# A two-block network on one core: split buffers, later transposes and a mirrored half inverse transform in the context branch

## The chip, the cores and the metric

One core of a Trainium2 chip runs the whole program. The time is device microseconds of one execution, all loads from HBM included. Lower is better.

## The reference

The network has two blocks, each of 256 positions by 1024 features, and a context of the same size beside each.

The first block has two layers. A layer is a token mixer (an mLSTM with four heads in two directions, a depthwise convolution of width 31 and a 2-D Fourier mix, each on a part of the projected features, then an output projection) and an expert layer, in which each of 16 experts takes its 32 best tokens:

```
xs = xn[idx]                                  # 32 tokens of each expert
hid = silu(xs @ w_gate[e]) * (xs @ w_up[e])
y[idx] += gate * (hid @ w_down[e])
```

In layer 0 the context stream goes through both parts as well; in layer 1 it only gives the mLSTM its start states.

The second block first runs a Hyena mixer, on the latents and, separately, on a second context `ctx_2`; then an attention over both. The Hyena mixer of one sequence h of length 256 is:

```
x0, x1, v, z = split(h @ w_in)   # the first three through a convolution of width 3
u = x1 * v
y = irfft(rfft(u, 512) * rfft(k, 512))[:256] + u * d_skip
out = (y * x0 * silu(z)) @ w_out
```

A gate, a shift and a scale for each part come from small vectors times the modulation matrices (`w_ada`, `ada_w_2`). Everything is in 32-bit floats.

## The kernel before

The class `K` writes out the program. `build` asks for a schedule by a simulated timeline (L1589): what the functions write is a program order with dependencies, and the order of the instructions on each engine, fixed when the program is built, may differ from it. Each engine then works its own list. DMA issues are in these lists as well: most on SyncE's queue (SP), those of the context branch on GpSimd's (POOL).

`run` (L1332) goes through these stages: the mixer of layer 0, its routing and experts (with the Hyena filters' spectra `Kd` made beside them), the mixer of layer 1, its routing (`route_tokens`, L701) and experts (`experts`, L825), the context branch of Hyena (`hyena` called with G = 1, `three` False), the latents' Hyena (G = 2, `three` True), attention. Layer 1's experts and the context branch don't depend on each other, so their instructions are interleaved.

An expert of layer 1 is 12 loads of 1 MB (`ew`, L884): four of `w_e_gate`, four of `w_e_up`, four of `w_e_down`. The first six loads go into buffers `W2`, the rest into the five buffers `W` that all stages share. Each load is used by 16 TensorE instructions (`expert_k`, L819) for M = 32 tokens. After gate and up, the hidden row `h` gets its silu on ScalarE and its product on VectorE, is transposed, and goes into the down projection of the same expert.

The context branch works through 16 tiles of 128 channels. For each tile it loads two blocks `Wb` of 1 MB, and makes four projections (`projT`, L266) in the order x1, v, x0, z. A projection splits the weight in two halves, and each half into `hi` (ScalarE cast) and `lo` (VectorE subtraction), with `sbufs` = 2 buffers each; three matmuls per row block (L109 to L111) multiply the pieces with the split input `hyx`, which is X2, the normalized and transposed `ctx_2`. After v, GpSimd forms the even and the odd half `uf` of u (L1058), TensorE transposes them (L1059), ScalarE copies them into `u`; a forward transform with `fe` (four 128-column products), products with the spectrum `Kt` on VectorE (`Yf`, `ht1`), and an inverse transform with `fi`: four products of 256 columns, summed in PSUM. Then `x0s` is multiplied by it and split into `hm`, and after each block of four tiles `out_proj` (L1098) multiplies by `hy_w_out`. The last block, tile 15, is held back until the 15th expert's silu (`late[14]`).

X2 is made inside the context branch (`modulated`, L1092), after the experts in program order. Its pools lie on the right side of the on-chip memory, where the pool of `W2` lay before them.

Modulation parts are named by place (`PLACES`, L28). "a1 b0 b1" are 16 loads of 1 MB of `ada_w_2`, written at `R1`, inside the routing of layer 1. Each load is used by eight TensorE instructions (L191).

Of the kernel before, what the change touches and what calls it, by code (L numbers as in the profile page):

```python
# [27 lines left out]
PLACES = dict(P0="", M0="01 02 10", L0="", R0="a0", W1="", P1="11", M1="12", L1="", R1="a1 b0 b1")  # L28
# [3 lines left out]
class K:  # L32
    def __init__(self, ctx, tc, A, out):
# [15 lines left out]
        self.wgate, self.late = [], {}  # L49

# [275 lines left out]
    def mixer(self, l, x, hc, cols, R, ada):  # L326
# [8 lines left out]
        with self.pool("nrm", tags=("xh", "xtmp")):  # L335
            for s, src in ((0, hc), (1, x)):
                xh = self.normed(src, "og" if s else "xh", 1)
                self.toT(xh, a1, cols[:, 0], s, xhi[:, :, s * 256:s * 256 + 256], xlo[:, :, s * 256:s * 256 + 256],
                         banks=("tp", "sm", "sm", "mm") if s else ("mm", "mm", "mm", "tp"))
# [5 lines left out]
        ott = [0, 1, 2, 3] if full else [2, 3]  # L345
        cum = []
# [78 lines left out]
        flo = T([128, 2, 2, 128], "flo")  # L425
        for s in streams:
# [14 lines left out]
            if s in om:  # L441
                Q[s] = self.parts([128, 1, 256], "Q", 2, True)
# [5 lines left out]
            if s in om:  # L448
# [3 lines left out]
                nc.scalar.activation(flo[:, s], pm, AF.Exp, scale=-1.0)  # L452
# [19 lines left out]
        sgc = T([128, 2, 512], "t4k", 2)  # L472
        ypad = T([128, 2, 2, 286], "ypad")
        nc.vector.memset(ypad[:, :, :, 0:15], 0.0)
        nc.vector.memset(ypad[:, :, :, 271:286], 0.0)
        for h in range(2):
            ps = self.P([128, 512])
            self.projT(ps[:, oc0:], chunk(1 + h), X, oc0, on)
            nc.scalar.activation(sgc[:, h, oc0:], ps[:, oc0:], AF.Sigmoid)
        for h in range(2):  # L480
            ps = self.P([128, 512])
            self.projT(ps[:, oc0:], chunk(3 + h), X, oc0, on)
            for s in om:
                nc.vector.tensor_tensor(ypad[:, h, s, 15:271], ps[:, s * 256:s * 256 + 256],
                                        sgc[:, h, s * 256:s * 256 + 256], op=OP.mult)

        cw, cbias = self.colv["cw", l], self.colv["cb", l]
        acc = T([128, 2, 2, 256], "t4k", 2)
        yo = slice(0, 2) if full else slice(1, 2)

        def terms():
            for j in range(31):
                for h in range(2):
                    av, yv = acc[:, h, yo], ypad[:, h, yo, j:j + 256]
# [10 lines left out]
        qT = T([128, 4, 512], "qT")  # L505
# [4 lines left out]
        for h in range(4):  # L510
            ps = self.P([128, 512])
            self.projT(ps[:, oc0:], chunk(9 + h), X, oc0, on)
            self.copy(qT[:, h, oc0:], ps[:, oc0:])
# [9 lines left out]
        fz = T([128, 4, 256], "t4k", 2)  # L523
# [3 lines left out]
        for q, t in enumerate(ott):  # L527
            self.copy(fz[:, t], pss[q])


        og = T([128, 4, 512], "og")
# [3 lines left out]
        for q, t in enumerate(ott):  # L535
            nc.scalar.activation(og[:, t], pss[q], AF.Sigmoid)
            nc.vector.tensor_tensor(og[:, t], og[:, t], ghn, op=OP.mult)
# [32 lines left out]
        mhi = T([128, 8, 512], "mhi", 1, F32R)  # L570
        mlo = T([128, 8, 512], "mlo", 1, F32R)
# [4 lines left out]
        for s in om:  # L576
            hh[s] = T([128, 4, 2, 128], "hh", 2)
            for h in range(4):
                pS = self.P([128, 2, 256])
                c0 = s * 256  # L580
                for t in range(2):
                    nc.tensor.matmul(pS[:, t], lhsT=kT[:, h, c0 + t * 128:c0 + (t + 1) * 128], rhs=qT[:, h, c0:c0 + 256],
                                     start=True, stop=True)
                for d in range(2):
# [13 lines left out]
                    if s == 1:  # L598
# [5 lines left out]
                        nc.vector.tensor_tensor(qs, qs, qT[:, h, 256:512], op=OP.mult)  # L604
# [12 lines left out]
                    nc.vector.tensor_tensor(rd, rd, flo[:, s, :, r], op=OP.max)  # L617
# [10 lines left out]
            for h in range(4):  # L628
                pt = self.PT([128, 256])
                for t in range(2):  # L630
                    nc.vector.scalar_tensor_tensor(hh[s][:, h, t], hh[s][:, h, t], rsh[:, s, h, t:t + 1],
                                                   og[:, 2 * s + t, h * 128:(h + 1) * 128], op0=OP.mult, op1=OP.mult)
                    nc.tensor.transpose(pt[:, t * 128:(t + 1) * 128], hh[s][:, h, t], self.ident)
                c0 = s * 256
# [4 lines left out]
        for h in range(2):  # L639
            po = self.PT([128, 512])  # L640
            for s in om:
                ps = self.PS([128, 512])
                for t in range(2):
                    nc.tensor.matmul(ps, lhsT=fz[:, 2 * s + t, h * 128:(h + 1) * 128], rhs=fw[:, t], start=(t == 0), stop=(t == 1))
# [5 lines left out]
            nc.scalar.copy(mhi[:, 6 + h, oc0:], po[:, oc0:])  # L650
            nc.vector.tensor_tensor(mlo[:, 6 + h, oc0:], po[:, oc0:], mhi[:, 6 + h, oc0:].bitcast(F32), op=OP.subtract)


        av = acc.rearrange("p h s t -> p h (s t)")[:, :, oc0:]
# [22 lines left out]
        for h in range(2):  # L677
            nc.scalar.activation(av[:, h], av[:, h], AF.Silu, bias=lb[:, h:h + 1], scale=lg[:, h:h + 1])
            nc.scalar.copy(mhi[:, 4 + h, oc0:], av[:, h])
            nc.vector.tensor_tensor(mlo[:, 4 + h, oc0:], av[:, h], mhi[:, 4 + h, oc0:].bitcast(F32), op=OP.subtract)  # L680
# [3 lines left out]
        for n in range(2):  # L684
# [3 lines left out]
            self.projN(wt, (mhi, mlo), ott, 512, pss)  # L688
# [913 lines left out]
```

## Time and profile before

| | |
|---|---|
| median of 3 runs | 2364.46 us (2359.9 to 2367.83) |
| profiled execution, its own time | 2366.99 us |
| its span, first to last instruction | 2365.2 us |
| mean granted clock of TensorE | 0.955 |
| bytes moved | 664.09 MB, 281 GB/s over the span |

The profile is of one execution. Times in a trace are microseconds from the start of its span. A row of the windows gives the busy time of each engine in a stretch, with the number of instructions, then the granted clock (1.00 is 2.4 GHz, 0.50 is 1.2 GHz), the mean busy share of the 16 DMA engines and the rate that they moved. Matmuls are pipelined, so the durations of neighbours overlap.

### The profile page before, as it was taken

The numbers are of one execution on the slowest core, as the hardware profiler recorded it, in microseconds if no ns is written. First come the engines' busy times: TensorE is split into PE (matmuls) and PEld (weight loads), VectorE is DVE, ScalarE is ACT, GpSimd is POOL, SyncE is SP. The second block draws the span as 40 slices with busy tenths as digits, with TensorE's granted clock in tenths as the row PEclk, the third lists the DMA queues.
The fourth block names the chain that finished last, engine by engine and source line by source line (L and its number), as shares of the span: only waits on it lengthen the run. The fifth ranks groups of instructions, "written<-read, shape, count | busy, mean of one in ns | idle before, by whom it ended". The sixth has DMA issues, their size and how long they took to land.

```text
span 2365.2 us, 35049 instructions
## 1 busy us (share of the span) xinstructions
PE 2135.7 (90%) x13966; PEld 1436.1 (61%) x13966; DVE 1250.4 (53%) x2533; ACT 737.5 (31%) x1414; POOL 187.7 (8%) x315
## 2 busy tenths in 40 slices
PE   5999988999999989998799998898777999999998
PEld 3776664343343436864376766665234999979786
DVE  3954444333433337654355555544125878875776
ACT  3323331000000014343233222222013555555665
POOL 1000000011010100000011011100001110100100
PEclk8999999999999999999899999998777999999999
DMA  8247545999999996459799999988996545435320
GB/s 342 99 157 312 204 184 193 413 415 415 414 413 415 414 405 251 137 194 370 295 351 365 372 374 370 351 336 327 421 421 262 185 144 188 168 132 189 126 81 26
DMA packets 129588, 664.09 MB, mean 281 GB/s; under 512 B 12666, under 2 KB 23429, under 8 KB 62352
## 3 DMA queue, kind: packets, MB, share of 16 engines
q1 hardware_dynamic: 115616, 602.89, 66.0%
q0 software_dynamic: 13808, 58.96, 6.6%
q8 instruction: 110, 1.80, 0.3%
q14 instruction: 54, 0.44, 0.1%
HBM read 656.56 MB, written 5.24 MB: 280 GB/s over the span
## 4 chain that ended last, share of the span: by engine, by line
PE 72%; DVE 9%; issue 8%; DMA 7%; ACT 3%; POOL 1%; SPq 0%; DVEq 0%; POOLq 0%; ACTq 0%
PE pmm L823 16%; PE pmm L109 12%; PE pmm L111 11%; PE pmm L110 11%; PE pad L191 3%; PE psm L875 2%; DMA W<-in_w_e_gate 1%; DVE lo L105 1%; DMA W<-in_w_e_up 1%; PE ptp L1017 1%; DMA W<-in_w_ada 1%; PE pmm L798 1%; PE pad L978 1%; DMA W<-in_ada_w 1%; PE ppo L1247 1%
## 5 line engine op out<-in xcount | busy, mean ns | idle before, releaser
L823 PE MATMUL pmm<-W,XS 128*32 128x256 f32 (+1 forms) x3040 | 378.8, 478 | 39.7 <-DMA W<-in_w_e_gate 20.3
L105 DVE TENSOR_TENSOR lo<-W,hi 128x512 fp32r<-128x512 f32 (+1 forms) x420 | 283.7, 680 | 187.1 <-ACT hi L104 184.2
L104 ACT CAST hi<-W 128x512 fp32r<-128x512 f32 (+1 forms) x420 | 255.5, 612 | 352.0 <-PE pmm L110 162.9
L823 PEld LDWEIGHTS pmm<-W,XS 128*32 128x32 f32 (+1 forms) x3040 | 127.0, 123 | 241.3 <-issue 151.1
L823 PE MATMUL pmm<-W,hT 128*32 128x256 f32 (+1 forms) x1536 | 190.1, 483 | 20.2 <-DVE hT L101 8.3
L111 PE MATMUL pmm<-hyx,lo 128*128 128x256 f32 x640 | 191.6, 299 | 10.6 <-DVE lo L105 10.6
L109 PE MATMUL pmm<-hyx,hi 128*128 128x256 f32 x640 | 193.4, 302 | 4.8 <-ACT hi L104 4.8
L110 PE MATMUL pmm<-hyx,hi 128*128 128x256 f32 x640 | 185.8, 290 | 0.0
L105 DVE TENSOR_TENSOR lo<-Wb,hi 128x512 fp32r<-128x512 f32 x160 | 109.4, 692 | 117.3 <-ACT hi L104 116.3
L104 ACT CAST hi<-Wb 128x512 fp32r<-128x512 f32 x160 | 96.8, 619 | 209.4 <-PE pmm L110 138.3
L869 DVE TENSOR_TENSOR Y<-pmm,gt 32x512 f32<-32x512 f32 (+1 forms) x128 | 70.9, 554 | 143.5 <-PE pmm L823 141.8
L109 PE MATMUL pmm<-hyl,hi 128*128 128x256 f32 x512 | 144.5, 283 | 1.7 <-DVE rtmp L697 1.7
L110 PE MATMUL pmm<-hyl,hi 128*128 128x256 f32 x512 | 144.1, 282 | 0.0
L111 PE MATMUL pmm<-hyl,lo 128*128 128x256 f32 x512 | 143.1, 283 | 0.0
L109 PEld LDWEIGHTS pmm<-hyx,hi 128*128 128x128 f32 x640 | 126.6, 198 | 23.7 <-ACT hi L104 16.6
L111 PEld LDWEIGHTS pmm<-hyx,lo 128*128 128x128 f32 x640 | 126.3, 197 | 22.3 <-DVE lo L105 14.1
L823 PEld LDWEIGHTS pmm<-W,hT 128*32 128x32 f32 (+1 forms) x1536 | 65.6, 125 | 117.6 <-issue 68.6
L110 PEld LDWEIGHTS pmm<-hyx,hi 128*128 128x128 f32 x640 | 126.6, 198 | 2.4 <-issue 2.2
L851 ACT ACTIVATE h<-pmm 128x256 f32<-128x256 f32 (+1 forms) x31 | 15.1, 488 | 362.1 <-PE pmm L823 361.9
L191 PE MATMUL pad<-W,cpad 128*32 128x512 f32 x576 | 91.0, 643 | 21.6 <-DMA W<-in_w_ada 16.7
L854 DVE TENSOR_TENSOR h<-h,pmm 128x512 f32<-128x512 f32 (+1 forms) x32 | 17.7, 552 | 171.9 <-ACT h L851 89.5
L109 PEld LDWEIGHTS pmm<-hyl,hi 128*128 128x128 f32 x512 | 97.4, 190 | 3.4 <-issue 1.9
(516 smaller groups left out, 4084.1 us busy)
## 6 DMA issues: line engine op xcount, KB each, us to landing
W<-in_w_e_gate SPq DMA_DIRECT2D x128, 1024.0 KB, 11.2
W<-in_w_e_up SPq DMA_DIRECT2D x128, 1024.0 KB, 11.2
W<-in_w_e_down SPq DMA_DIRECT2D x128, 1024.0 KB, 11.2
W<-in_w_ada SPq DMA_DIRECT2D x48, 1024.0 KB, 6.6
W<-in_hyw SPq DMA_DIRECT2D x32, 1024.0 KB, 5.1
Wb<-in_hyw POOLq DMA_DIRECT2D x30, 1024.0 KB, 8.9
W<-in_ada_w SPq DMA_DIRECT2D x24, 1024.0 KB, 5.2
W<-in_at_w_in SPq DMA_DIRECT2D x16, 1024.0 KB, 5.0
```

Source lines behind the costliest of these rows:

```text
L104: self.nc.scalar.copy(hi, w)
L105: self.nc.vector.tensor_tensor(lo, w, hi.bitcast(F32), op=OP.subtract)
L109: mm(out, lhsT=l[0], rhs=r[0], start=start, stop=False)
L110: mm(out, lhsT=l[0], rhs=r[1], start=False, stop=False)
L111: mm(out, lhsT=l[1], rhs=r[0], start=False, stop=stop)
L191: nc.tensor.matmul(ps[32 * j:32 * j + 32, :], lhsT=self.cpad[:, blk, k0 + k, :], rhs=wt[:, k, j * 512:(j + 1) * 512], start=(k0 + k == 0), ...
L798: nc.tensor.matmul(ps, lhsT=v, rhs=S[s][:, t], start=(t == 0 and q == 0), stop=(t == 1 and q == 1))
L823: self.nc.tensor.matmul(ps[M * j:M * j + M], lhsT=v, rhs=wt[:, j * N:(j + 1) * N], start=(k == 0), stop=(k == 7))
L869: nc.vector.tensor_tensor(Y[s][32 * r:32 * r + 32, c], py[p0:p0 + 32], gt[s][p0:p0 + 32, c], op=OP.mult)
L875: nc.tensor.matmul(ps, lhsT=SgT[s][:, q, t * 128:(t + 1) * 128], rhs=Y[s][:, n * 512:(n + 1) * 512], start=True, stop=True)
L978: nc.tensor.matmul(ps[:, i, f], lhsT=self.fd[:, t, i * 256 + f * 128:i * 256 + (f + 1) * 128], rhs=ab[:, i, t], start=(t == 0), stop=(t == 1))
L1017: self.nc.tensor.matmul(out, lhsT=l[0], rhs=r[0], start=start, stop=stop)
```

## The change

Seven edits, six of them in the stretch from the mixer of layer 1 to the end of the context branch:

- The context branch has four split buffers (`sbufs` = 4), except while `between` runs.
- The transposes of `uf` come after the projection of x0 (`q == 2`), not directly after v. The inverse transform with what follows it (`back`) and a block's output projection are put in a list `pend`, and are written after the projection of v of the next tile (`flush`). The latents' branch writes all of it at once, as before.
- In the context branch the inverse is computed for the first 128 positions only, the even part (cosines) and the odd part (sines) apart; their sum gives these positions, their difference, read backwards, the other 128. `fi` is loaded with 128 columns.
- In layer 1 the transposes and the down projection of expert e are written after gate and up of expert e + 1.
- `W2` has four buffers in layer 1, not six, and lies on the left side.
- X2 is made at the end of the mixer of layer 1, in a pool of its own (`x2`), and "a1 b0 b1" moves to `L1` (a step beside each head and direction of the mLSTM, the rest ahead of the output projection).
- The tiles of the mixer have in layer 1 the size that one stream needs. `split` stands for the same two instructions where they were written out.

The core of the diff (the tile sizes of the mixer left out):

```diff
-PLACES = dict(P0="", M0="01 02 10", L0="", R0="a0", W1="", P1="11", M1="12", L1="", R1="a1 b0 b1")
+PLACES = dict(P0="", M0="01 02 10", L0="", R0="a0", W1="", P1="11", M1="12", L1="a1 b0 b1", R1="")
...
-        F2.enter_context(self.pool("w2", tags=("W2",)))
+        F2.enter_context(self.pool("w2", "right" if ns == 2 else "left", tags=("W2",)))
...
+        put_off = ns == 1
+
+        def down(e, hv):
+            q, r = divmod(e, 4)
+            pt = self.PT([128, nS, 128])
...
             nc.vector.tensor_tensor(hv, hv, pgu[1], op=OP.mult)
...
+            if put_off and e:
+                down(e - 1, last)
+            last = hv
+            if not put_off:
+                down(e, hv)
+        if put_off:
+            down(15, last)
...
-            r = (self.ecount - 1) % 10 if ns == 2 else 11 - self.ecount
+            r = (self.ecount - 1) % 10 if ns == 2 else 9 - self.ecount
             if ns == 1 and r >= 5:
-                t = self.T([128, 2, 1024], "W2", 6)
+                t = self.T([128, 2, 1024], "W2", 4)
...
-            fe, fi = T([128, 2, 256], "fe"), T([128, 4, 256], "fi")
+            fe, fi = T([128, 2, 256], "fe"), T([128, 4, 128], "fi")
...
-                x0s = T([128, G, 256], "x0s", G)
+                x0s = T([128, G, 256], "x0s", 2)
...
-                                pt = self.PT([128, 2, 128])
                                 uf = T([128, 2, 128], "uf", 2)
                                 for c, op in enumerate((OP.add, OP.subtract)):
                                     nc.gpsimd.tensor_tensor(uf[:, c], cv[1][:, :128], cv[1][:, 128:][:, ::-1], op=op)
-                                    nc.tensor.transpose(pt[:, c], uf[:, c], self.ident)
-                                self.put([v[:, :, i * 128:(i + 1) * 128] for v in u], pt)
+                                if not three:
+                                    self.flush()
...
+                        if q == (1 if three else 2):
+                            pt = self.PT([128, 2, 128])
+                            for c in range(2):
+                                nc.tensor.transpose(pt[:, c], uf[:, c], self.ident)
+                            self.put([v[:, :, i * 128:(i + 1) * 128] for v in u], pt)
...
-                Yf = T([128, 2, 2, n], "Yf", HB["Yf"] if three else 1)
+                Yf = T([128, 2, 2, n], "Yf", HB["Yf"] if three else 2)
...
+                self.pend.append(lambda Y=Y, x0s=x0s, m=m, i0=G * g - g0: self.back(Y, x0s, m, i0, blocks[0][1]))
+                if three:
+                    self.flush()
+            self.pend.append(lambda m=m, g0=g0, wg=wg: self.out_proj(x, A["hy_w_out_2"][0], m, g0, wg, gt, dma,
+                                                                     wg - G if three and g0 + wg == 16 else 0))
+            if three:
+                self.flush()
+        self.flush()
...
+    def back(self, Y, x0s, m, i0, width):
+
+        G = x0s.shape[1]
+        if not m:
+            m += self.parts([128, width, 256], "hm", 1, True)
+        py = self.PT([128, G, 256])
+        if len(Y) == 1:
+
+            for c in range(2):
+                for f in range(2):
+                    self.mmx(py[:, 0, c * 128:(c + 1) * 128], [v[:, c, f] for v in Y], [v[:, 2 * c + f] for v in self.fis],
+                             f == 0, f == 1)
+            y = self.T([128, 2, 128], "yh", 1)
+            ye = self.T([128, 128], "ye", 1)
+            nc = self.nc
+            nc.scalar.copy(ye, py[:, 0, :128])
+            nc.vector.tensor_tensor(y[:, 0], ye, py[:, 0, 128:], op=OP.add)
+            nc.vector.tensor_tensor(y[:, 1], ye[:, ::-1], py[:, 0, 128:][:, ::-1], op=OP.subtract)
+            y = y.rearrange("p a b -> p (a b)")[:, None]
...
+        self.nc.vector.tensor_tensor(x0s, x0s, y, op=OP.mult)
+        self.split(x0s, *[v[:, i0:i0 + G] for v in m])
...
                 self.wgate = [self.late[15]] * 5
+                adm.enter_context(self.pool("x2", tags=("hyx0", "hyx1")))
                 with self.pool("m1"):
                     self.mixer(1, x, hc, m1[1], m1[0], ada)
+
+                    c2 = self.load_x("ctx_2", "hc")
+                    a0 = self.modA(b0[1], 1, self.colv["ng", 0], "a1")
+                    X2 = self.modulated(c2, a0, b0[1][:, 0], 1, xh="W", side="left")
...
                         self.wtag, self.wbufs = "Wb", 2
-                        c2 = self.load_x("ctx_2", "hc")
+                        self.sbufs = 4
                         self.hy_consts(False)
-                        a0 = self.modA(b0[1], 1, self.colv["ng", 0], "a1")
                         gtc = self.row_bcast(b0[0][:, 0], 0, 64, 1, "gtc", 1)
-                        X2 = self.modulated(c2, a0, b0[1][:, 0], 1)
```

## Rows read from the trace of the kernel before

**Rows 1.** The page, busy time and share of each engine over the span.

```profile
PE 2135.7 (90%) x13966; PEld 1436.1 (61%) x13966; DVE 1250.4 (53%) x2533; ACT 737.5 (31%) x1414; POOL 187.7 (8%) x315
```

**Rows 2.** Windows: bounds, length, busy PE, PEld, DVE, ACT, POOL, clock, DMA share, GB/s.

```profile
1000.00:1044.00 44.00, 43.09 (x267) 30.29 (x266) 25.85 (x84) 20.65 (x56) 0.00 (x0) 1.00 0.57 219
1044.00:1101.00 57.00, 53.08 (x254) 29.02 (x252) 22.99 (x48) 16.28 (x33) 3.29 (x5) 0.94 0.76 276
1101.00:1140.00 39.00, 27.42 (x131) 15.82 (x131) 22.26 (x58) 11.48 (x18) 0.90 (x2) 0.82 0.80 328
1140.00:1186.00 46.00, 30.64 (x347) 13.47 (x346) 10.13 (x21) 10.66 (x20) 5.09 (x9) 0.83 0.84 336
1186.00:1640.00 454.00, 415.06 (x3712) 309.71 (x3712) 242.47 (x480) 131.01 (x253) 45.36 (x79) 0.97 0.92 355
1640.00:1762.00 122.00, 82.00 (x824) 32.99 (x823) 16.07 (x32) 4.04 (x9) 0.30 (x2) 0.74 1.00 413
```

**Rows 3.** Waits of SyncE's queue, 1140 to 1800: total, times, longest.

```profile
SPq L895 <- PE pmm L823: 527.2, 177, 32.6
```

**Rows 4.** Waits of TensorE, 1186 to 1640: total, times, longest.

```profile
PE pmm L111 <- DVE lo L105: 10.6, 11, 1.7
PE ptp L1059 <- POOL uf L1058: 7.1, 9, 1.4
PE pmm L110 <- DVE lo L105: 5.7, 3, 2.7
PE pmm L109 <- ACT hi L104: 4.6, 7, 1.5
PE psm L1017 <- ACT u L1011: 2.3, 5, 0.5
PE pmm L823 <- ACT hT L99: 2.1, 3, 0.7
PE ptp L1017 <- DVE Yf L1077: 2.0, 2, 1.4
...
PE ptp L1017 <- issue: 1.2, 1, 1.2
...
PE ptp L857 <- DVE h L854: 0.9, 1, 0.9
```

**Rows 5.** Timeline of TensorE: start, duration, line, shape, count.

```profile
1075.52 1.06 PE L191 MATMUL pad<-W,cpad 128*32 128x512 f32 x8
...
1204.46 1.16 PE L1017 MATMUL psm<-u,fe 128*128 128x128 f32 x8
1205.55 1.07 PE L823 MATMUL pmm<-W,XS 128*32 128x256 f32 x16
1207.85 1.10 PE L1017 MATMUL ptp<-fi,Yf 128*128 128x256 f32 x4 [1.23 <-issue]
...
1209.02 1.03 PE L1017 MATMUL ptp<-fi,Yf 128*128 128x256 f32 x4
```

**Rows 6.** Timeline, two copies of 128x129 from PSUM.

```profile
1039.05 0.29 DVE L101 COPY C<-ptp 128x129 f32<-128x129 f32 x1
...
1040.24 0.28 ACT L99 COPY C<-ptp 128x129 f32<-128x129 f32 x1
```

**Rows 7.** Expert matmuls by operand, 1186 to 1640: count, busy, mean ns.

```profile
L823 PE MATMUL pmm<-W,XS 128*32 128x256 f32 x1152 | 75.9, 385 | 0.0
L823 PE MATMUL pmm<-W,hT 128*32 128x256 f32 x640 | 41.2, 384 | 3.1 <-ACT hT L99 2.1 <-DVE hT L101 1.0
```

**Rows 8.** Timeline of GpSimd, 880 to 1260.

```profile
1146.49 0.61 POOL L992 DMA_DIRECT2D fe<-in_fe  x1 [40.86 <-PE pmm L823]
```

**Rows 9.** Timeline of ScalarE, 1140 to 1192.

```profile
1164.77 0.62 ACT L104 CAST hyx<-xtmp 128x512 fp32r<-128x512 f32 x1
1184.94 0.38 ACT L851 ACTIVATE h<-pmm 128x256 f32<-128x256 f32 x1 [19.56 <-PE pmm L823]
1185.22 1.13 ACT L104 CAST hi<-Wb 128x512 fp32r<-128x512 f32 x2
```

More of the change, by code (lines that the diff above doesn't have):

```diff
@@ L345, in mixer @@
         ott = [0, 1, 2, 3] if full else [2, 3]
+        s0 = 0 if full else 1
         cum = []
@@ L836, in experts @@
         Y = {}
+        put_off = ns == 1
+        def down(e, hv):
+            q, r = divmod(e, 4)
+            pt = self.PT([128, nS, 128])
+            for i in range(nS):
+                nc.tensor.transpose(pt[:, i], hv[:, i * 128:(i + 1) * 128], self.ident)
+            hT = T([128, 4, 128], "hT", 2)
+            self.copy(hT[:, :nS], pt)
+            py = self.P([128, N])
+            for k in range(8):
+                j, i = divmod(k, nS)
+                self.expert_k(py, A["w_e_down"][l, e], k, [hT[:, i, M * j:M * j + M]] * G, M, N, ns)
+            if r == 0:
+                Y.update({s: T([128, 1024], "Y", ns) for s, _ in xs})
+            for i, (s, x) in enumerate(xs):
+                for jj in range(G):
+                    p0, c = M * jj + 32 * i, slice(jj * N, (jj + 1) * N)
+                    nc.vector.tensor_tensor(Y[s][32 * r:32 * r + 32, c], py[p0:p0 + 32], gt[s][p0:p0 + 32, c], op=OP.mult)
+            if r == 3:
+                for s, x in xs:
+                    for t in range(2):
+                        for n in range(2):
+                            ps = self.PS([128, 512])
+                            nc.tensor.matmul(ps, lhsT=SgT[s][:, q, t * 128:(t + 1) * 128], rhs=Y[s][:, n * 512:(n + 1) * 512],
+                                             start=True, stop=True)
+                            xv = x[:, t, n * 512:(n + 1) * 512]
+                            nc.vector.tensor_tensor(xv, xv, ps, op=OP.add)
         for e in range(16):
-            q, r = divmod(e, 4)
             pgu = []
@@ new lines, in hyena, with flush @@
+            if three:
+                self.flush()
+        self.flush()
+    def flush(self):
+        p, self.pend = self.pend, []
+        for f in p:
+            f()
+    def back(self, Y, x0s, m, i0, width):
[15 more added lines that the diff above has]
+            y = y.rearrange("p a b -> p (a b)")[:, None]
+        else:
+            for i in range(G):
+                for q in range(4):
+                    c, f = divmod(q, 2)
+                    self.mmx(py[:, i], [v[:, c, f, i * 128:(i + 1) * 128] for v in Y], [v[:, q] for v in self.fis], q == 0, q == 3)
+            y = py
+        self.nc.vector.tensor_tensor(x0s, x0s, y, op=OP.mult)
+        self.split(x0s, *[v[:, i0:i0 + G] for v in m])
@@ L1093, in modulated @@
+    def modulated(self, x, a, b, s, tag="hyx", banks=("tp", "mm"), xh="xh", side="right"):
         X = (self.T([128, 8, 256], tag + "0", 1, F32R), self.T([128, 8, 256], tag + "1", 1, F32R))
-        with self.pool("xn", tags=("xh", "xtmp")):
+        with self.pool("xn", side, tags=("xh", "xtmp")):
             self.toT(self.normed(x, xh, 1), a, b, s, *X, banks=banks)
@@ L1340, in run @@
         if True:
-            with self.psum("ps0", mm=4, tp=1, sm=2, ad=1):
+            with self.psum("ps0", sm=2, tp=1, mm=4, ad=1):
                 self.setup()
```

108 lines of the change are left out of this document (38 added, 70 removed).

## Prediction

> **What bounds the kernel now.** I read the page's busy line first: TensorE is busy 90% of the span, VectorE 53%, ScalarE 31% [rows 1]. That is an average over stages, so the next view is busy time cut at the borders of the stages that the diff touches [rows 2]. The reader should see three regimes after the second mixer. From 1186 to 1640 us the context branch of the Hyena block runs between the experts of layer 1: TensorE is busy 415.1 of 454 us at a granted clock of 0.97, while the DMA moves 355 GB/s. From 1640 to 1762 the experts are alone: 413 GB/s at a DMA share of 1.00, TensorE idle a third of the time and at a clock of 0.74. From 1140 to 1186 TensorE is busy only 30.6 of 46 us. So the joint stage is bound by TensorE, and the tail behind it by the transfers. Expert loads do not run ahead in the joint stage because their buffers are freed late: SyncE's queue waited 527.2 us in 177 waits for expert matmuls (from 1140 to 1800) [rows 3]. Whatever lets TensorE get through the joint stage faster lets expert weights in faster.
>
> What TensorE lacks in the joint stage is in the view of its waits [rows 4]: three rows for the split pieces hi and lo (10.6 + 5.7 + 4.6 = 20.9 us), three for the transforms (7.1 for uf from GpSimd, 2.3 for u, 2.0 for Yf) and 1.2 of issue ahead of the inverse transform, together 12.6; 2.1 + 0.9 = 3.0 for the experts' hidden activations. No wait for a DMA is among them.
>
> **The change part by part.** Inverse transform on half the positions. A channel tile now issues eight instructions of 256 columns (1.10 + 1.03 us for the two runs of four) [rows 5]. After the change they have 128 columns, and the forward transform has just that shape: eight in 1.16 us. That is 0.97 us a tile, and 14.6 us over the 15 tiles of the joint stage; as matmul durations overlap at their ends I take 12, with 0 and 14.6 as the ends. The Trainium skill (TensorE: Matmul & The Clock Gate, LDWEIGHTS) says that a weight load's time goes with its columns, about 107 ns for 128, and (Back-to-back issue gap) that weight loads share in setting the spacing of small matmuls; that speaks against half the columns being half the time, and by it alone (an estimate from the page) the eight could not go below 0.85 us. The trace agrees: 1.16 is more than half of 2.13. The added work is one ScalarE copy and one more VectorE operation of 128x128, and the nearest rows cost 0.28 and 0.29 us [rows 6]; about 0.6 to 0.9 us a tile, hidden behind TensorE, since VectorE is busy 242 and ScalarE 131 of the 454 us [rows 2]. Without that cover it would be 13 us.
>
> Four split buffers. With two, a cast into hi has to wait for the matmuls that read the piece before last. With four the splits can run two pieces ahead. Ends: none or all of the 20.9 us; I take two thirds, 14, since each engine's order is fixed when the program is built, and a split can still stand behind something late.
>
> Later transposes and the put-off back half. The transposes of uf come after the projection of x0, and the inverse of tile g after the second projection of tile g+1, so that TensorE has matmuls that depend on none of it. Ends 0 and 12.6; two thirds is 8.4. The experts' down projection put off by one expert: 0 to 3.0, taken as 2. In the tail it is worth nothing, as the weights set the pace there. The joint stage would go from 454 to 454 - 12 - 14 - 8.4 - 2 = 418 us.
>
> What of this is given back. The joint stage holds 1792 expert matmul instructions [rows 7], 16 to a load of 1 MB, so 112 loads. Such a load costs TensorE 1.07 us there [rows 5], but in the tail 1.049 MB / 413 GB/s = 2.54 us. A load pushed from the joint stage into the tail costs 1.47 us net. If the scheduler keeps the number of expert loads per channel tile, nothing is pushed. If it keeps their pace in time (112 in 454 us), n loads are pushed where 112 - n = 0.247 x (418 - 1.07 n), n = 12, and 18 us are given back. I take the middle, 9.
>
> Earlier X2. Now the context constants overlay the experts' extra buffers: the first GpSimd load of fe waits 40.86 us for expert matmuls, until 1146.5 [rows 8]. X2 then has its last cast at 1164.8, and the first weight split follows only at 1185.2 [rows 9]. After the change X2 is made during the second mixer, and the extra buffers lie on the other side, so the context can start once the routing tiles are free, near 1140. TensorE idles 15.4 us between 1140 and 1186 [rows 2]. Ends 0 and 15; I take 6, because the DMA is already busy and a channel tile's loads delay expert loads. The skill (DMA: Bandwidth & Descriptors, Issuing engines are not separate DMA queues) says the same of loads issued by GpSimd and SyncE; the share of 1.00 in the tail is the limit here.
>
> Fewer extra buffers (four, not six). Two loads less are fetched ahead during routing, 2 x 2.54 = 5 us at most; I take 3.
>
> The modulation loads a1, b0, b1 (16 of 1 MB) move from routing into the second mixer, ahead of the loads of w_out on SyncE's queue. Their matmuls cost about 1.06 us a load [rows 5], 17 us in all; in the trace they already run between 1044 and 1112 us, where TensorE is busy 53.1 of 57 us, and they would go into the heads, where it is busy 43.1 of 44 [rows 2]. Work moves from one full stretch to another. The heads become some 15 us longer, the stretch after them as much shorter; w_out waits behind 16 loads. 0, with 8 us either way. The smaller tiles of mixer 1 change no instruction, and the latent Hyena block is issued as before.
>
> Sum: -36 + 9 - 6 + 3 = -30 us. The profiled execution took 2366.99 us (span 2365.2), 2.5 above the median of the runs, 2364.46; 2337 for it, so 2334 for the median.
>
> **The rivals.** (1) The transfers become the bound. From 1140 to 1762 the bytes are 46 x 336 + 454 x 355 + 122 x 413, that is 227 MB; at 413 GB/s they take 550 us in place of 622, 72 less: about 2295. For it: the upper ends of the terms (14.6 + 20.9 + 12.6 + 3.0 + 15) add up to 66. Against it: TensorE must then wait for almost nothing.
>
> (2) The order decides, and nothing can be measured. X2's last cast ended at 1165.4, and the splits still came 20 us later, directly behind an expert activation that ScalarE had waited 19.56 us for [rows 9]. If the new order keeps such places, less than half of the 36 us comes, and the pace rule and the lost buffers take it: about 2360. The skill's rule for it (TensorE: Matmul & The Clock Gate, Architectural detail) is that ScalarE and VectorE work their queues strictly first in, first out; those two rows agree.
>
> (3) Slower: the context branch gets so dense that too many expert loads are pushed into the tail. Place: the tail; price 1.47 us a load; it decides from (36 + 6 - 3) / 1.47 = 27 loads on, that is when the joint stage holds 85 instead of 112. At 35 loads it gives +12, 2376. For it: every part of the change makes the context branch quicker for the scheduler and none makes expert weights quicker. Against it: it needs more than twice the 12 loads of the pace rule.
>
> **How the numbers follow.** Forecast (12 to 52 us faster, own range 2312 to 2352) 0.55; rival 1 0.12; a gain between 7 and 12 us 0.10; rival 2 0.11; rival 3 0.12. A change of 0.3%, 7 us, is about what a measurement of this kernel can tell from none. So faster 0.77, same 0.11, slower 0.12. The range goes from rival 1 to just short of rival 3, 2294 to 2364.
>
> **What would show it.** In the trace after: the inverse runs with 128 columns at about 1.16 us for eight; TensorE's waits for hi, lo and uf in the joint stage fall below 15 us; the first hyx matmul comes before 1160; the joint stage moves over 380 GB/s; the tail stays near 413 GB/s and has 48 (122 x 413 / 1.049) to 60 expert loads. I am wrong if the tail grows by more than 27 loads, if waits for DMA appear in the joint stage, or if the mixer ends over 8 us later.

## The result and the profile after

The changed kernel took 2381.35 us in the median of 4 runs (2381.07 to 2383.82), the kernel before 2362.96 us beside it (4 runs). The ratio of the two is 1.0073, with a 95% interval of 1.0058 to 1.0087: 18 us slower. The forecast was 2334 us, with a range of 2294 to 2364. The profiled execution has a span of 2382.0 us, against 2365.2.

The windows of the kernel after, cut at the same events as [rows 2]: the mixer in two parts, routing up to the first expert matmul, up to the first hyx matmul, the joint stage, and the tail up to tile 15.

```profile
1000.00:1062.00 62.00, 61.83 (x377) 35.39 (x379) 26.89 (x85) 20.01 (x53) 0.00 (x0) 1.00 0.86 328
1062.00:1114.00 52.00, 47.84 (x200) 31.91 (x198) 28.98 (x62) 23.20 (x47) 4.19 (x7) 0.87 0.56 202
1114.00:1151.00 37.00, 21.72 (x89) 14.04 (x93) 21.58 (x55) 11.69 (x18) 2.82 (x5) 0.77 0.38 149
1151.00:1170.00 19.00, 14.29 (x168) 6.26 (x168) 1.11 (x2) 5.18 (x9) 2.14 (x4) 0.82 0.76 293
1170.00:1588.00 418.00, 384.39 (x3437) 294.67 (x3437) 240.00 (x499) 127.35 (x263) 43.50 (x79) 0.97 0.92 345
1588.00:1764.00 176.00, 117.71 (x1180) 41.97 (x1178) 21.14 (x44) 3.74 (x10) 0.30 (x2) 0.75 1.00 414
```

The stretch from there to the latents' Hyena (its first matmul on `hyl`) is not in [rows 2], so here are both kernels, the window of before first.

```profile
1762.00:1820.00 58.00, 43.24 (x318) 26.54 (x317) 34.65 (x60) 22.29 (x39) 6.04 (x12) 0.76 0.85 333
```

```profile
1764.00:1838.00 74.00, 52.27 (x399) 31.83 (x400) 37.16 (x66) 22.77 (x42) 4.58 (x10) 0.77 0.87 342
```

The reader is to see that the joint stage shrank as forecast, from 454 to 418 us, and that the time came back elsewhere. Against [rows 2] the first expert starts 11 us later (1151 for 1140); the wait for the context falls from 46 to 19 us (-27); joint stage -36; tail +54 (176 for 122); the stretch behind it +16 (74 for 58). The sum is +18, which is 1838 against 1820. Behind that point nothing changed: 2382.0 - 1838 = 544 us, and 2365.2 - 1820 = 545.

What the tail took over is in the counts of expert matmuls, joint stage first, then tail; 16 make one load of 1 MB (columns as in [rows 7], then the idle time before them and what ended it).

```profile
L824 PE MATMUL pmm<-W,XS 128*32 128x256 f32 x1008 | 67.7, 387 | 0.0
L824 PE MATMUL pmm<-W,hT 128*32 128x256 f32 x512 | 34.0, 385 | 0.0
...
L824 PE MATMUL pmm<-W,XS 128*32 128x256 f32 x768 | 71.9, 512 | 37.1 <-DMA W<-in_w_e_gate 20.1 <-DMA W<-in_w_e_up 17.1
L824 PE MATMUL pmm<-W,hT 128*32 128x256 f32 x384 | 36.2, 512 | 19.5 <-DMA W<-in_w_e_down 19.5
```

The same rows of the tail before, 1640 to 1762:

```profile
L823 PE MATMUL pmm<-W,XS 128*32 128x256 f32 x528 | 46.4, 489 | 25.7 <-DMA W<-in_w_e_up 15.1 <-DMA W<-in_w_e_gate 10.6
L823 PE MATMUL pmm<-W,hT 128*32 128x256 f32 x256 | 23.0, 520 | 6.7 <-DMA W<-in_w_e_down 4.6 <-DVE hT L101 1.0 <-ACT hT L99 1.0
```

The joint stage holds 1520 / 16 = 95 loads in place of 112 [rows 7], the tail 1152 / 16 = 72 in place of 784 / 16 = 49. By the same view 160 / 16 = 10 loads come ahead of the joint stage in place of 320 / 16 = 20, and 240 / 16 = 15 behind the tail in place of 176 / 16 = 11; each kernel adds up to 192. In the tail TensorE waits for weights. The loads that went past the tail are in the 16 us behind it: the DMA moved 74 x 342 = 25.3 MB there, in place of 58 x 333 = 19.3 MB.

TensorE's waits in the joint stage, 1170 to 1588, against [rows 4].

```profile
PE ptp L1028 <- DVE Yf L1092: 10.2, 10, 2.3
PE pmm L112 <- DVE lo L106: 7.4, 10, 1.4
PE ptp L1078 <- POOL uf L1068: 5.4, 6, 2.1
PE pmm L110 <- ACT hi L105: 3.3, 5, 1.3
PE pmm L111 <- DVE lo L106: 2.0, 1, 2.0
```

hi and lo fell from 20.9 to 12.7 us, uf from 7.1 to 5.4, together 18.1 where below 15 was forecast; Yf rose from 2.0 to 10.2.

The inverse transform in that stage, before and after:

```profile
L1017 PE MATMUL ptp<-fi,Yf 128*128 128x256 f32 x120 | 34.1, 408 | 3.2 <-DVE Yf L1077 2.0 <-issue 1.2
```

```profile
L1028 PE MATMUL ptp<-fi,Yf 128*128 128x128 f32 x120 | 20.2, 295 | 11.1 <-DVE Yf L1092 10.2 <-PE pmm L824 0.6
```

And SyncE's queue around routing (start, time over which the loads were issued, loads):

```profile
1012.83 48.04 SPq L187 DMA_DIRECT2D W<-in_ada_w  x16
1061.36 9.04 SPq L321 DMA_DIRECT2D W<-in_w_out  x4
1082.49 24.19 SPq L906 DMA_DIRECT2D W<-in_w_e_up  x4
1112.55 46.21 SPq L906 DMA_DIRECT2D W<-in_w_e_gate  x8
```

The 16 modulation loads are now done by 1061, and with four extra buffers little is left for the DMA in routing: 149 GB/s from 1114 to 1151, where it was 328 [rows 2].

**One way to read it.** The bytes from 1000 us to the latents' Hyena are the same: 820 x 347 and 838 x 339 are both 284 to 285 MB. So the stretch is longer by the time that the DMA lost below its rate. The fastest long stretch of any run moved 421 GB/s; the lost time of a window is its length x (1 - rate / 421).

| lost DMA time, us | before | after |
|---|---|---|
| from 1000 to the first hyx matmul | 58.6 | 70.4 |
| joint stage | 71.2 | 75.5 |
| tail | 2.3 | 2.9 |
| to the latents' Hyena | 12.1 | 13.9 |
| sum | 144.2 | 162.7 |

The difference is 18.5 us. With equal bytes it has to be the difference in length, so the table shows where the 18 us lie, and not what caused them. 15.3 of it arose in routing alone (8.6 to 23.9), of which the earlier start of the context gave back 3.5 (9.3 to 5.8). The joint stage is 36 us shorter and yet lost 4 us more.

### The profile page after: what moved, and what is told of

It is laid out like the page before. It is cut to its first block, busy times and chain, and to the rows that moved or that the text cites. A ratio compares the mean times of both kernels' runs of the same rounds, so it can differ in the third digit from the quotient of the medians.

```text
span 2382.0 us, 34984 instructions
## 1 busy us (share of the span) xinstructions
PE 2140.9 (90%) x13955; PEld 1435.1 (60%) x13966; DVE 1253.7 (53%) x2565; ACT 735.8 (31%) x1430; POOL 185.0 (8%) x315
## 4 chain that ended last, share of the span: by engine, by line
PE 34%; issue 9%; DVE 5%; ACT 1%; DMA 1%; POOL 1%; SPq 0%; DVEq 0%; POOLq 0%; ACTq 0%
PE pmm L112 8%; PE pmm L111 7%; PE pmm L110 7%; PE pmm L824 3%; DVE lo L106 1%; PE ppo L1295 1%; POOL uf L1068 1%; PE poo L111 1%; PE poo L112 1%; PE poo L110 1%; PE psm L1028 1%; PE ptp L1028 1%; PE ptp L1290 1%; DMA Wb<-in_hyw 0%; DVE Yf L1090 0%
## 5 line engine op out<-in xcount | busy, mean ns | idle before, releaser
L824 PE MATMUL pmm<-W,XS 128*32 128x256 f32 (+1 forms) x3040 | 387.2, 489 | 43.2 <-DMA W<-in_w_e_gate 26.1
L824 PE MATMUL pmm<-W,hT 128*32 128x256 f32 (+1 forms) x1536 | 195.9, 490 | 35.4 <-DMA W<-in_w_e_down 26.1
L105 ACT CAST hi<-Wb 128x512 fp32r<-128x512 f32 x160 | 90.2, 618 | 60.4 <-PE pmm L111 43.5
```

The costliest lines, as they stand in the source:

```text
L105: self.nc.scalar.copy(hi, w)
L824: self.nc.tensor.matmul(ps[M * j:M * j + M], lhsT=v, rhs=wt[:, j * N:(j + 1) * N], start=(k == 0), stop=(k == 7))
```

## The experiments

They stand in the order in which they ran. An expectation names its theories itself, or takes them from the one ahead. "Joint stage" is always the stretch from the first hyx matmul to the tail. A ratio is that of a version's time to the kernel before, measured beside it (medians of 2363.8 to 2365.1 us), with its 95% interval. One load is 16 expert matmuls, as above.

**The move of the modulation loads.** The kernel after with a1, b0, b1 back in routing, and the kernel before with only the move:

```
# e1 (in the kernel after); e2 is the reverse, in the kernel before
-PLACES = dict(..., L1="a1 b0 b1", R1="")
+PLACES = dict(..., L1="", R1="a1 b0 b1")
```

> The kernel after, with the 16 modulation loads a1 b0 b1 back in the routing (R1); all else as after. Theory A (the move leaves the DMA idle late in the mixer and in the routing, and makes the experts start 10 to 13 us later): the mixer's last matmul comes back from 1114 to about 1101, the time falls by 10 to 15 us, to 2366 to 2371. Theory B (the loss is that the denser context branch pushes expert loads into the tail; the late start is made good there, as the bytes behind it are the same): 2378 to 2384, with 20 or more loads more in the tail than before.

Measured 2369.27 us, ratio to before 1.0023 (1.0013 to 1.0032): 12 us less than after, as theory A said. Routing moved 344 GB/s (1100 to 1144). But its tail holds (752 + 384) / 16 = 71 loads, 22 more than before, as theory B said, and it is only 5 us slower than before.

> The kernel before, with only the 16 modulation loads moved to the second mixer (L1). Theory A: 10 to 15 us slower than before, 2373 to 2378, with a DMA rate under 200 GB/s in the routing. Theory B: no change that can be measured, 2359 to 2367.

Measured 2356.87, ratio 0.9975 (0.9961 to 0.9988): the move alone is a gain of some 6 us, which neither theory forecast, although routing fell to 196 GB/s. Its joint stage, in a profiled execution of 2351.28 us:

```profile
1188.00:1624.00 436.00, 406.27 (x3701) 301.39 (x3702) 241.30 (x478) 130.76 (x254) 44.67 (x79) 1.00 0.94 368
```

With 111 loads in it, as before, that stage is 18 us shorter, and TensorE's waits for uf fell from 7.1 to 0.9 us, though nothing was edited there. TensorE's instructions stand in another order there than before. So the move has no price of its own; what it costs hangs on the order that the rest gets.

**Holding the context at its weight loads.** The first `Wb` load of a channel tile waits until ScalarE has done the silu of the expert before:

```
+if not three and q == 0 and ct >= 1:
+    self.after(wt[0:1, 0, 0, 0:1], self.late[min(ct - 1, 14)])
```

> The kernel after, with each tile of the context branch held back: the first weight load of tile g (g from 1 on) waits for the silu of expert g - 1, so that the branch cannot run ahead of the experts. Theory B: the joint stage then has some 140 expert loads in place of 95, TensorE is shared more evenly with the loads, the DMA stays near 400 GB/s to the end and the time falls by 30 to 50 us, to 2331 to 2351. Theory A: the order in which the two branches share TensorE is not what costs; within 5 us of after, 2376 to 2386, or slower by what the held back loads stall on GpSimd's queue.

Measured 2387.87, ratio 1.0104 (1.0087 to 1.0121). Tiles are held, but each now pays for its load: TensorE's and ScalarE's waits, 1391 to 1846.

```profile
PE pmm L110 <- ACT hi L105: 41.2, 7, 10.9
```

```profile
ACT hi L105 <- DMA Wb<-in_hyw: 111.0, 8, 17.1
```

> The kernel before with the same holding back of its context tiles. Theory B: the joint stage had 112 expert loads at 355 GB/s; paced it has some 140, and the time falls by 20 to 45 us, to 2318 to 2343. Theory A: within 5 us of before, or slower.

Measured 2368.82, ratio 1.0025 (1.0015 to 1.0035). Its context is spread, with 12 loads to each tile from the fourth on, and TensorE's wait for hi, 1183 to 1800, is up from 4.6 us [rows 4]:

```profile
PE pmm L109 <- ACT hi L104: 67.5, 14, 9.5
```

Holding the load is the wrong place: the split stands in ScalarE's list and waits for a transfer that is issued too late.

**Parts one by one.** In the kernel after, no put-off:

```
-        put_off = ns == 1
+        put_off = False
```

> The kernel after, with the experts' transposes and down projections in their old place (not put off by one expert). Theory T (TensorE time in the joint stage buys time): 2 to 6 us slower than after, 2383 to 2388. Theory D (what makes the joint stage shorter comes back in the tail): within 4 us of after. Theory P (putting the down projection off is itself the loss, since the loads of down of expert e come behind eight loads of expert e + 1 and the last experts end later): faster by 8 or more, under 2374, and fewer than 15 loads behind the first matmul of tile 15.

Measured 2367.13, ratio 1.0015 (1.0006 to 1.0024): 14 us less than after, as theory P said. The joint stage takes 406 us, 95 loads, 356 GB/s, and 11 loads come behind the first matmul of tile 15 in place of 15.

In the kernel after, two split buffers in the context branch (`self.sbufs = 2`):

> The kernel after, with two split buffers in the context branch in place of four. Theory T: the waits for hi and lo return to some 20 us and the time rises by 8 to 15 us, 2389 to 2396. Theory D: the joint stage gets longer by that, with 6 to 12 expert loads more in it and as many less in the tail; within 6 us of after, or faster.

Measured 2370.13, ratio 1.0016 (1.0001 to 1.0032). Joint stage and tail:

```profile
1165.00:1617.00 452.00, 411.51 (x3728) 305.73 (x3732) 250.02 (x508) 133.77 (x268) 46.76 (x79) 0.97 0.92 360
1617.00:1752.00 135.00, 89.84 (x895) 31.98 (x888) 16.36 (x35) 4.05 (x10) 0.30 (x2) 0.73 1.01 419
```

The joint stage is 34 us longer than after's and holds 113 loads again; the tail is 41 us shorter. Theory D had the direction right, with 6 to 12 loads where 18 came.

In the kernel before, only the half inverse (the code in short, not word for word):

```
-fi = T([128, 4, 256], "fi")          # four products of 256 columns, summed
+fi = T([128, 4, 128], "fi")          # four of 128 columns, two sums:
+y[:, 0] = ye + yo                    # ye copied from PSUM by ScalarE
+y[:, 1] = reversed(ye) - reversed(yo)
```

> The kernel before, with only the inverse transform of the context branch on half the positions. Theory T: the joint stage loses 12 us of TensorE and the time falls by 8 to 14 us, to 2350 to 2356. Theory D: the joint stage is 10 us or more shorter, with fewer expert loads in it and more in the tail, and the time is within 4 us of before.

Measured 2358.35, ratio 0.9989 (0.9977 to 1.0): 3 us faster by the ratio, 5 by the medians, and the interval just includes no gain. The joint stage stays at 454 us with 113 loads, so neither theory's mechanism is seen. The wait for uf rose from 7.1 [rows 4] to:

```profile
PE ptp L1059 <- POOL uf L1058: 16.6, 14, 3.1
```

In the kernel before, only four split buffers (`self.sbufs = 4` ahead of `hy_consts`):

> The kernel before, with only four split buffers in place of two in the context branch. Theory T: the waits of TensorE for hi and lo fall from 20.9 us to under 8 and the time falls by 10 to 15 us, to 2349 to 2354. Theory D: the waits fall, but the joint stage then holds fewer than 105 expert loads and the time is within 4 us of before, or above.

Measured 2364.76, ratio 1.0009 (0.9998 to 1.0019). Joint stage and tail, and the expert matmuls of each:

```profile
1184.00:1591.00 407.00, 384.11 (x3430) 293.49 (x3434) 235.31 (x471) 127.00 (x250) 41.54 (x79) 1.00 0.93 350
1591.00:1754.00 163.00, 100.96 (x1092) 37.01 (x1092) 18.03 (x39) 3.74 (x10) 0.30 (x2) 0.79 1.00 416
```

```profile
L823 PE MATMUL pmm<-W,XS 128*32 128x256 f32 x996 | 68.8, 385 | 0.0
L823 PE MATMUL pmm<-W,hT 128*32 128x256 f32 x512 | 32.8, 384 | 1.9 <-DVE hT L101 1.4 <-ACT hT L99 0.5
...
L823 PE MATMUL pmm<-W,XS 128*32 128x256 f32 x688 | 63.3, 505 | 37.3 <-DMA W<-in_w_e_gate 20.5 <-DMA W<-in_w_e_up 16.8
L823 PE MATMUL pmm<-W,hT 128*32 128x256 f32 x384 | 29.6, 444 | 16.4 <-DMA W<-in_w_e_down 13.3 <-DVE hT L101 1.6 <-ACT hT L99 1.5
```

One edit shows what takes the gain back: the joint stage is 47 us shorter, 94 loads are in it in place of 112, 67 in place of 49 in the tail, which is 41 us longer, and the time is the same.

**Holding the context at its split.** The weights of a tile are loaded as early as ever; its first split into hi waits for the silu of the expert before, by a copy of one number that the split overwrites. The gate of tile 15's load is dropped.

```
 def projT(self, ps, w, x, c0, n, gate=None):
...
+    if gate is not None and k0 == 0:
+        self.nc.scalar.copy(hi[0:1, 0, 0:1], gate)
...
+held = not three and q == 0 and ct >= 1
+projT(ps, wt[:, q % 2], X, 0, 256, self.late[min(ct - 1, 14)] if held else None)
```

> The kernel after with the modulation loads back in the routing, and with the context tiles held back once more, but at the first split and not at the load: ScalarE copies one number of expert g - 1's silu into the first hi tile of context tile g, so that the weights are on chip when the tile is let go. Theory O (the order fixed at build decides how many expert loads the joint stage holds; where the holding is without a wait for a load, the DMA is used evenly): the waits of TensorE for hi that cost e3 41 us fall under 15, and the time is 15 to 40 us under that of e1, 2329 to 2354. Rival N (the time goes with the bytes and with the stretches in which the DMA idles anyway; spreading the context only moves them): within 6 us of e1, 2363 to 2375, or slower.

Here it stands in e1's kernel. Measured 2337.29, ratio 0.9888 (0.9863 to 0.9913), as theory O said. TensorE's waits for hi are 8.7 us from 1163 to 1740, where e3 had 41.2.

> The kernel before with its context tiles held back at the first split. Theory O: 15 to 40 us faster than before, 2324 to 2349. Rival N: within 6 us of before, or slower.

In the kernel before: 2338.08, ratio 0.9891 (0.9867 to 0.9914). There is hardly a tail left; the stretch up to 1750 holds (1760 + 896) / 16 = 166 loads:

```profile
1183.00:1750.00 567.00, 511.45 (x4724) 356.14 (x4724) 275.22 (x541) 144.27 (x290) 48.13 (x82) 0.95 0.97 389
```

**Two gains together.** e2's move and e8's half inverse in the kernel before:

> The kernel before with the modulation loads moved to the second mixer (as e2, 7 us faster than before) and the inverse transform on half the positions (as e8, 5 us faster). If the two gains are each their own: 2349 to 2354. If what e2 and e8 gained is the luck of another order of instructions: anywhere from 2355 to 2370.

Measured 2380.04, ratio 1.0067 (1.0046 to 1.0088). Two edits, one a gain and one about nothing, cost 16 us together, more than either theory allowed. The joint stage takes 466 us, and uf is waited for again:

```profile
PE ptp L1059 <- POOL uf L1058: 16.1, 15, 2.1
```

**The put-off alone** in the kernel before (the expert loop of after):

> The kernel before, with only the experts' transposes and down projections put off by one expert. Theory P (putting off costs by itself, as e6 was 14 us faster than after): 8 to 15 us slower than before, 2371 to 2379, with 15 loads behind the first matmul of tile 15 in place of 11. Rival S (every edit reshuffles the order in the joint stage, worth 10 us either way): 2357 to 2370.

Measured 2367.66, ratio 1.0015 (1.0001 to 1.0029): 15 loads come behind the first matmul of tile 15, as theory P said, but they cost 3.5 us and not 8 to 15.

**Four extra buffers** in the kernel before (`W2` of 4, not 6):

> The kernel before, with only four extra buffers W2 in layer 1 in place of six. Two loads less are on chip when the experts start: 5 us slower if it only shifts the loads, 2366 to 2371; within 3 us if the loads that come later are hidden by the wait for TensorE in the joint stage. Theory S would put up to 10 us on it either way, to be read from the joint stage and not from the routing.

Measured 2371.18, ratio 1.0033 (1.0021 to 1.0046): +7 us. Routing moves 275 GB/s in place of 328, which is 4.9 us of lost DMA time more, close to the price of two loads; the joint stage is 11 us longer as well (465), with 16.1 us of waits for uf:

```profile
1096.00:1135.00 39.00, 27.36 (x138) 15.70 (x140) 22.44 (x58) 11.52 (x19) 0.90 (x2) 0.87 0.67 275
```

**The split gate in the kernel after**, the move kept:

> The kernel after as it is (modulation loads in the second mixer), with the context tiles held back at the first split as in e10. If the move of the loads costs by itself (the experts start 7 us later and the routing leaves the DMA idle), it is 5 to 10 us slower than e10, 2342 to 2348. If its cost in the kernel after was mostly the order in the joint stage, it is within 3 us of e10, 2334 to 2340. In both cases the DMA moves 390 GB/s or more while the context runs, and the loss of the kernel after against before is gone.

Measured 2339.1, ratio 0.9905 (0.9885 to 0.9925). Routing still runs at 152 GB/s; the stretch from 1169 to 1735 moves 400. The intervals of e16 and e10 overlap, so a cost of the move by itself is not seen here.

**The split gate, later.** e10 with tiles 1 to 7 waiting for one expert more (`late[ct]`):

> As e10, but tiles 1 to 7 wait for one expert more (tile g for the silu of expert g). In e10 the DMA is still under 350 GB/s from 1180 to 1240, while two context tiles run behind each other. If holding them back fills that stretch, 3 to 6 us faster than e10, 2331 to 2334; if the same shortfall comes back where tiles 7 and 8 follow each other, within 3 us of e10.

Measured 2336.16, ratio 0.9885 (0.9871 to 0.9898): the same as e10, so the rival holds.

**An edit that changes no work.** In the kernel before, the loads of fe and fi in the other order:

> The kernel before, with one edit that has no work in it: the loads of fe and fi, two constants of the context branch, are written in the other order. Theory S (any edit gives another order of instructions in the joint stage, and the order alone is worth some us): the wait of TensorE for uf in the joint stage, 7.1 us before, is another one (0 to 17), and the time differs from before by up to 12 us either way. Rival (an edit without work changes nothing): within 3 us of before, the same waits.

Measured 2363.37, ratio 1.0000 (0.9989 to 1.0011); the waits of the joint stage are those of before. TensorE's 4516 matmuls from the first hyx matmul to tile 15 stand in the same order in both traces. So not every edit reshuffles the order.

**The inverse products made twice** in the kernel before (each result is computed a second time; the output is the same):

```
-                for i in range(G):
+                for i in list(range(G)) * (1 if three else 2):
```

> The kernel before with work added: in the context branch the four products of the inverse transform are made twice (the second set overwrites the first with the same numbers), 120 matmul instructions and some 20 to 30 us of TensorE more in the joint stage. If TensorE's time there is what sets the kernel's time: 20 to 30 us slower, 2384 to 2394. If the expert loads keep their pace of about 0.25 in a us whatever TensorE has to do: the joint stage gets longer by 25 us or more, with 6 or more expert loads more in it and as many less in the tail, and the time rises by under 10 us, to 2364 to 2374.

Measured 2365.93, ratio 1.0007 (0.9998 to 1.0016). Joint stage and tail:

```profile
1183.00:1640.00 457.00, 432.66 (x3842) 325.19 (x3846) 243.48 (x480) 130.85 (x253) 46.66 (x79) 0.99 0.91 352
1640.00:1759.00 119.00, 78.81 (x800) 27.98 (x797) 14.91 (x31) 2.89 (x8) 0.30 (x2) 0.73 1.01 421
```

The inverse of that stage, against 34.1 us before:

```profile
L1017 PE MATMUL ptp<-fi,Yf 128*128 128x256 f32 x240 | 56.8, 384 | 7.5 <-DVE Yf L1077 6.2 <-issue 1.2
```

The stage holds its 112 loads and ends where it did. TensorE's busy time rose by 17.6 us, and its idle time fell from 38.9 to 24.3. The inverse alone added 22.7; the rest of the work took 5 us less, at a granted clock of 0.99 where it was 0.97. The time lies in the second range of the expectation, but its mechanism, more loads in a longer stage, did not come.

**The best of it.** The kernel before with the half inverse, four split buffers and the split gate:

> The kernel before (six extra buffers, modulation loads in the routing), with the half inverse, four split buffers and the context tiles held back at the first split. With the context paced, loads no longer leave the joint stage, so that what is saved on TensorE should show at last: 2 to 8 us under e11, 2330 to 2336. If the transfers are already the bound there, within 2 us of e11, 2336 to 2340.

Measured 2333.97 (2330.12 to 2334.49), ratio 0.9867 (0.9855 to 0.988), the fastest version, 30 us under before:

```profile
1185.00:1749.00 564.00, 500.52 (x4724) 351.93 (x4723) 279.44 (x573) 144.96 (x306) 44.34 (x82) 0.93 0.97 390
```

The half inverse and the four buffers add some 4 us to the gate's gain by the medians; the interval overlaps that of e11, so this is not shown.

The counts side by side, all without a gate (e14 and e20, with two split buffers, hold 114 each):

| split buffers | kernel | joint stage, us | loads in it |
|---|---|---|---|
| 2 | before | 454 | 112 |
| 2 | e2 | 436 | 111 |
| 2 | e7 | 452 | 113 |
| 2 | e8 | 454 | 113 |
| 2 | e12 | 466 | 113 |
| 2 | e13 | 465 | 113 |
| 2 | e22 | 457 | 112 |
| 4 | after | 418 | 95 |
| 4 | e1 | 413 | 96 |
| 4 | e6 | 406 | 95 |
| 4 | e9 | 407 | 94 |

Not the time sets how many loads fit in, but the order: about 112 / 15 = 7.5 loads a channel tile with two split buffers, whether the stage takes 436 or 466 us, and 6.3 with four. Tile by tile, TensorE's list has mostly 6 loads between the first projections of neighbours and some 12 at the end of a block of four with two split buffers, and mostly 5 and some 10 with four. This list is fixed when the program is built, so no event of the run can change the count.

## Why the prediction was wrong

**The step that failed** is "Whatever lets TensorE get through the joint stage faster lets expert weights in faster", and with it the term of what is given back. It allowed 0 to 18 us and took 9, with half of the pace rule's 12 loads pushed into the tail. 23 were: 17 out of the joint stage and 10 that had been ahead of it, less 4 that went past the tail. They go with a tail 54 us longer, 2.35 us each, close to the 2.54 used. e9 and e7 show it from both sides, each with no other edit: four split buffers take 47 us from the joint stage in one and 34 in the other, and put 41 into the tail in both. The pushed loads take the gain back, and little more: e1 has 22 more in its tail than before and is 5 us slower, e9 has 18 more and takes the same time. e22 shows the other half: 18 us more TensorE work in the joint stage cost nothing that could be measured. TensorE was 91% busy there and still not what set the time.

What the runs point to in its place is the DMA below its rate, at 0.92 of its share, held by buffers that come free in the order fixed when the program is built. The split gate adds a copy of one number to a tile, drops the gate of tile 15's load, and otherwise changes only that order; the DMA then moves 389 GB/s in place of 355, and 26 us go out of the kernel before (e11). Spreading the context is not enough by itself: e4 has as many loads to a tile, but TensorE waits for hi, and nothing is gained. That a change of the order can be worth 26 us is shown; that it works by way of the idle DMA is argued from these runs.

**Inverse half**, -12: on TensorE it measured 34.1 - 20.2 = 13.9 us, so the size was right; in time it is worth 3 to 5 us, with an interval that just includes no gain (e8). Halving the columns brings a product from 408 to 295 ns, not to half. Eight take 20.2 / 15 = 1.35 us, a little over the 1.16 of the forward transform. The Trainium skill's statement that weight loads share in the spacing of small matmuls (TensorE: Matmul & The Clock Gate, Back-to-back issue gap) agrees with that. The 1.35 us change nothing in the time.

**Four split buffers**, -14: the waits for hi and lo fell by 8.2 us after, by 11.8 alone (e9: 9.1 left in its view). In time that was worth nothing (e9).

**Later transposes and the put-off**, -8.4 and -2: the waits that they should shorten were 12.6 us in sum before, and after uf and Yf alone make 15.6: the wait moved to the next step, Yf. Taking the put-off away made the kernel after 14 us faster (e6); put alone into the kernel before it costs 3.5 us (e14). It was forecast as a small gain.

The joint stage's 418 us came out as forecast, then, partly by the wrong road: 17 loads out of it are 17 x 1.07 = 18 us of TensorE work, half of the 36, and the inverse is 14. TensorE's idle time, which three of the terms were to shorten by 14 + 8.4 + 2 = 24 us, fell by 5 (38.9 to 33.6).

**Earlier X2**, -6: the first hyx matmul came at 1170, not before 1160, as the context's constants had to wait for the routing's last transposes until 1148; the wait behind the first expert fell by 27 us, more than the 15 allowed. But 10 loads that used to come ahead of the context now come behind it. e1 has the same early context (1163) and reaches the latents' Hyena at 1822, where before did at 1820: no gain is left there. X2 was not moved alone, so what it is worth by itself is not shown.

**Fewer extra buffers**, +3 (0 to 5): +7 alone (e13). The two loads cost 4.9 us in routing, within the range; the longer joint stage of e13 was not in the term.

**The move of the modulation loads**, 0 with 8 either way: 12 us in the kernel after (e1), -6 alone (e2), and 2 with the gate, which the noise covers (e16 against e10). Routing lost 15 us of DMA time in the kernel after; e6 and e7 lose as much there (150 GB/s each) and end 11 to 14 us earlier; their joint stages lose 10 to 13 us less. So the loss is real in its place, and whether the kernel pays for it hangs on what comes later. Mixer 2 ended 13 us later, over the 8 that were named as a sign of error.

**The rivals.** Rival 3 named the place and the mechanism, the tail and its pushed loads; 23 of them is short of its break-even of 27, which counted on a full gain of 36; with the 18 us that were not pushed loads, its own sum gives (18 + 6 - 3) / 1.47 = 14. The routing's loss came on top. Rival 1, the transfers as the bound, was wrong for this change: the rate in the joint stage fell to 345 GB/s. With the gate it comes to 389 to 400, and the time to 2334 to 2339. Rival 2's "the order decides" is what the counts show, but not so that every edit changes it (e20). The pace rule, a fixed number of loads per us, fell too: the number goes by the tile.

**What stays open.** Taking any one of three unlike parts out of the kernel after (e1, e6, e7) brings 11 to 14 us, more than 18 in sum, and e12 loses 16 us by two edits that each cost nothing. In joint stages without the gate the waits for uf run from none (e6, e9) to 16.6 us (e8). The granted clock differs too, 1.00 in e2 and 0.95 in e12; but of the 30 us between these two stages TensorE's busy time is only 9 (406 and 415), and the rest is waiting. Why the build-time order falls one way or the other was not settled; that it does, and that the gate takes most of it away (e10, e11, e16, e18 and e23 lie within 6 us of each other), is shown. That four buffers go with fewer loads per tile is shown; why the order gives them fewer was not looked into. The earlier X2, the later transposes with `pend`, the side of `W2` and the tile sizes of the mixer were never run alone.

## What to carry to other kernels

Where a compute-heavy branch is interleaved with a stream of weights by an order fixed at build time, count the loads per step of the branch and the time in which the DMA runs below its rate over the whole stretch; a busy engine, even at 91%, is no proof of the bound, and doubling a piece of its work is a cheap test. Price an edit of the filler branch only after asking how many loads go with each of its steps. Hold the filler to the pace of the stream, at a point where its own data are already on the chip, and not at its loads.

## What the runs showed of the hardware that was not expected

TensorE took 18 us more work in a stage where it was already busy 415 of 454 us, and the stage grew by 3 us (e22). The granted clock was 0.95 (e12) to 1.00 (e2, e9) over the joint stages without a gate, and 0.72 to 0.80 over their tails, in which TensorE waited for weights; the tails' rate was 413 to 421 GB/s all the same.
